# The scans' diagonal and levels 1, 2 and 4 computed between the products of the paired projections

## The chip, the core and the metric

The kernel runs on one core of a Trainium2 chip. A core has five engines that work side by side and wait for each other through semaphores: TensorE (PE in the profile, with its weight loads as PEld), VectorE (DVE), ScalarE (ACT), GpSimd (POOL) and SyncE (SP, which here only issues transfers). TensorE writes into PSUM, eight banks of 128 x 512 floats. Everything else lies in SBUF (128 partitions) or in DRAM. The metric is the time of one execution on the device in microseconds.

## The reference: what is computed

One inference step of a backbone with one layer, over 128 context tokens and 1024 latent tokens (1152 in all), with a model width of 1024. After a normalisation and one input projection there are two branches: a gated linear recurrence in both directions over 8 heads (key and value width 128), and a Fourier mixing of 4 channel groups. Both are gated, projected, merged and projected once more. The part that matters here is the recurrence and what feeds it:

```python
q, ff, fb, vi, zA, u, zB, gA, gB = jnp.split(proj, SPLITS, axis=-1)
qh = jax.nn.silu(heads(q))
logf_f, k_f = forget_gate(heads(ff), lb_f)      # f = lb + (1 - lb) * sigmoid(x), k = 1 - f
logf_b, k_b = forget_gate(heads(fb), lb_b)
o_f, S_f = hgrn2_chunk_scan(qh, logf_f, k_f, vh, s0_f)
o_b_rev, S_b = hgrn2_chunk_scan(qh[:, ::-1], logf_b[:, ::-1], k_b[:, ::-1], vh[:, ::-1], s0_b)
...
S_t = diag(f_t) S_{t-1} + k_t v_t^T,   o_t = S_t^T q_t
```

## The kernel before

**Stages.** Up to about 165 us the input is normalised and split into a high and a low part (three products with reduced operands stand for one product in full precision). Then come, with the v projection ahead, the paired projections: `pair(n, ...)` computes two blocks of 128 output channels for all tokens at once, in Strassen's scheme, with 7 products for 8. After these come the scans, one head after another, mixed with the gated projections of the two branches; then the rest of those and the output projection.

**A pair.** `pair` loads the weights of two blocks (`raw`, 1 MB in two transfers), builds seven operands from them (a11, s1, s2, s3, a12, a22, s4), each split by a cast on ScalarE (L525) and a subtraction on GpSimd (L526); three sums between them run on VectorE (L538 to L546). For each half `j` of the tokens TensorE runs the seven products of 12 matmuls each, 168 in a pair, into banks handed out in turn from six ("doo"), and VectorE adds the products together into `u1`, `u2`, `u3` and the results `ca`, `cb` (L551). What is done with a result depends on the block: `silu` (sigmoid on ScalarE, product on GpSimd), `forget` (sigmoid on ScalarE, L592, then a scale and an offset on GpSimd, L593), `silu_gain` (its product is on VectorE, L588). A transfer of SP takes each result to DRAM: `q_dr`, `f_dr` (both directions of the gate), `gz_dr`, `g_dr` and others. The pairs come in the order u (2 pairs), the heads (16 pairs: q with the forward gate, then the backward gate with zA), zB (2 pairs), gA with gB (7 pairs).

**The Fourier branch between the pairs.** `fourier()` is a generator of 20 steps, each a few small matmuls into the two banks of tag "s" with their copies. `pair` calls one step after each half from the third pair on (L573), so it runs in pairs 3 to 12. The program is written in this order with priorities, and a scheduler places the instructions of each engine; each engine then runs its own list in order.

**The scans.** For each head `load_head` brings the gates `ff` (128 x 2 x 1152) and `q`. `scan_blocks` makes kk = 1 - f and qq = q f, and then the part of the attention inside blocks of 32 tokens, in six steps: the diagonal (m = 0) and the levels m = 1, 2, 4, 8, 16. In a level the halves of kk and qq that belong together are copied side by side by ScalarE into `km` and `qm` (L686, L688); TensorE multiplies them in 36 blocks of 32 x 32 tokens (L695); VectorE merges the result into `a32` under a mask (L700; L698 for the diagonal); and `grow` (L660) multiplies kk and qq by the gates of the neighbouring blocks and joins these gates two by two, in place, in three instructions on VectorE (two of L665, one of L667). `scan_rest` goes on from there with levels 32 and 64, the states `S` from chunk to chunk (L767), the read-out and its norm. `PATTERN` gives the order of steps for each head by letters: E a step of `scan_blocks`, L and Y steps of `scan_rest` of the head before and the one before that, V half a chunk of the late v products, F half a block of the branch projections `dense`. In this stage `matmul` also ties TensorE's list to the order of the program.

Of the kernel before, what the change touches and what calls it, by code (L numbers as in the profile page):

```python
# [11 lines left out]
F32 = mybir.dt.float32  # L12
# [36 lines left out]
PATTERN = ['VVVVEEVVVEVVVEVVEVVEVV', 'LEVLEVLLEVVLLEFEFLLLEF', 'LFEFYYYFLEFLLEFLLEFEFLLLEFF', 'LEYYYFLEFLLEFLLEFEFLLLEFF', 'LEFYYYFLFELLEFLLEFEFLLLEFF', 'LEFYYYFLEFLLEFLLEFEFLLLEFF', 'LEFYYYFLFELLEFLLEFEFLLLEFF', 'ELFYYYFLEFLLEFLLEFEFLLELFF', 'LYYFYFLFLLFLLFLLLFFF', 'YFYYFFF']  # L49
HW = T // 2  # L50
SW = HW // 2
# [9 lines left out]
def diffusion_step(ctx: ExitStack, tc: tile.TileContext, xT, x_tok, w_pr, w_v, w_ada, w_ada_gt,  # L61
# [22 lines left out]
    q_dr = dram.tile([NH, P, T], F32, name="q_dr")  # L84
    f_dr = dram.tile([NH, P, 2, T], F32, name="f_dr")
# [349 lines left out]
    def load_head(p, hd):  # L435
        ff = p.tile([P, 2, T], F32, name="ff")
        nc.sync.dma_start(ff, f_dr[hd])
        q = p.tile([P, T], F32, name="q")
        nc.sync.dma_start(q, q_dr[hd])
        return ff, q  # L440


    def fourier():
        ct = lp.tile([P, T], F32, tag="vt", name="ct")
# [73 lines left out]
    four = fourier()  # L518

    with pool("se", 1) as se, pool("sl", 1) as sl_, pool("sp", 1) as sp:  # L520
# [8 lines left out]
        def pair(n, evacs):  # L529
# [6 lines left out]
            sb = sp.tile([P, 4, P], F32, name="sb")  # L536
# [5 lines left out]
            nc.vector.tensor_tensor(out=sb, in0=a11, in1=a21, op=ALU.subtract)  # L542
            w[7] = split(sb, "s3")
# [9 lines left out]
            for j in range(2):  # L553
                js = slice(j * SW, (j + 1) * SW)
                m = {}
                for i in (1, 5, 6, 7, 4, 2, 3):
                    m[i] = any_ps()[:, :SW]
                    mm3(m[i], [(w[i][0][:, k, :], w[i][1][:, k, :], mov[i][k][0][:, js], mov[i][k][1][:, js])
                               for k in range(4)])
                m1, u1, u2, u3 = (se.tile([P, SW], F32, name=x) for x in ("m1", "u1", "u2", "u3"))  # L560
# [12 lines left out]
                if n > 2:  # L573
                    next(four, None)
# [15 lines left out]
        def forget(i):  # L590
            def ev(c, j):
                nc.scalar.activation(c, c, AF.Sigmoid)  # L592
                nc.gpsimd.tensor_scalar(out=c, in0=c, scalar1=omlb[:, i:i + 1], scalar2=lb[:, i:i + 1], op0=ALU.mult,  # L593
                                        op1=ALU.add)

            return ev
# [27 lines left out]
        yf01 = lp.tile([P, 2, T], F32, tag="ff", name="yf01")  # L624
# [3 lines left out]
        for j in range(1, KT):  # L628
            pair(n, ((sigmoid, g_dr[0, j]), (sigmoid, g_dr[1, j])))
            n += 1  # L630
        first = load_head(lp, 0)
# [28 lines left out]
    def grow(ff, kk, qq, m):  # L660
        kk2, qq2, ff2 = (x.rearrange("p d t -> p (d t)") for x in (kk, qq, ff))
        dims = [[2 * m, T // (2 * m)], [T + m, 2], [1, m]]
        for x, off, step in ((qq2, T + m, -(T + m)), (kk2, m, T - m)):
            xv = view(x, 0, dims)
            nc.vector.tensor_tensor(out=xv, in0=xv, in1=view(ff2, off, [[2 * m, T // (2 * m)], [step, 2], [0, m]]), op=ALU.mult)  # L665
        fv = [view(ff2, o, [[T, 2], [2 * m, T // (2 * m)]]) for o in (0, m)]
        nc.vector.tensor_tensor(out=fv[0], in0=fv[0], in1=fv[1], op=ALU.mult)  # L667

    def scan_blocks(hd, ff, q):
        kk = s0[hd % 2].tile([P, 2, T], F32, name="kk")  # L670
        k0 = s0[0].tile([P, T], F32, tag="km", name="k0", bufs=2)
        qq = s0[hd % 2].tile([P, 2, T], F32, name="qq")
        a32 = s0[hd % 2].tile([P, NCH, 32], F32, name="a32")


        for d in range(2):
            nc.scalar.activation(kk[:, d, :], ff[:, d, :], AF.Identity, bias=ones[:, 0:1], scale=-1.0)
            nc.vector.tensor_tensor(out=qq[:, 1 - d, :], in0=q, in1=ff[:, d, :], op=ALU.mult)  # L678
        nc.vector.tensor_tensor(out=k0, in0=kk[:, 0, :], in1=kk[:, 1, :], op=ALU.add)
        kk2, qq2 = (x.rearrange("p d t -> p (d t)") for x in (kk, qq))  # L680
        for m in (0,) + LEVELS:
            ps = scan_ps()
            if m:
                dims = [[2 * m, T // (2 * m)], [T + m, 2], [1, m]]
                km = s0[0].tile([P, T], F32, name="km", bufs=2)
                nc.scalar.copy(km.rearrange("p (b i m) -> p b i m", i=2, m=m), view(kk2, 0, dims))  # L686
                qm = s0[0].tile([P, T], F32, name="qm", bufs=1)
                nc.scalar.copy(qm.rearrange("p (b i m) -> p b i m", i=2, m=m), view(qq2, 0, dims))  # L688
                grow(ff, kk, qq, m)
            else:  # L690
                km, qm = k0, q
# [10 lines left out]
            if m == 16:  # L702
                heads[hd] = (ff, kk, qq, a32)
# [400 lines left out]
```

## Time and profile before

| what | us |
|---|---|
| median of the runs (3) | 1366.0 |
| lowest and highest | 1364.75, 1376.12 |
| the profiled execution's own time | 1369.38 |
| its span | 1367.6 |
| PE busy in the span | 1257.8 (92%) |
| DVE busy | 853.0 (62%) |
| ACT busy | 569.4 (42%) |
| POOL busy | 658.7 (48%) |

The profile is of one execution on the chip. Each busy time is an average over stages that have different limits, so it is to be read by stage, as the slices of the page show. A row has 40 slices of 34.2 us, each digit is a busy share in tenths (9 is 90% or more), and PEclk is the clock that TensorE was granted, in tenths of full speed.

```profile
PE   5999899999999999999999996878787787999998
DVE  7737744444344344444443478999999999675554
POOL 4426546555647456558643503321312734464654
PEclk8899999999999999999999998898988898999999
```

The paired projections are the slices 5 to 23 or so, the scans 24 to 34. In a row of a timeline the columns are the start and the duration in us, the engine, the line, the operation with output and inputs, and in brackets how long the engine was idle before and what released it. In a row of a group the columns are the count, the busy time, the mean duration of one in ns and the idle time ahead of it. In a row of a tile the three numbers are the shortest, the median and the longest duration in ns. In a row of waits they are the total, the number of waits and the longest. Matmuls overlap, so a duration of 0.29 us stands for a matmul that starts 0.13 us after the one before it.

### The profile page before, as it was taken

The numbers are of one execution on the slowest core, as the hardware profiler recorded it, in microseconds if no ns is written. First come the engines' busy times: TensorE is split into PE (matmuls) and PEld (weight loads), VectorE is DVE, ScalarE is ACT, GpSimd is POOL, SyncE is SP. The second block draws the span as 40 slices with busy tenths as digits, with TensorE's granted clock in tenths as the row PEclk, the third lists the DMA queues.
The fourth block names the chain that finished last, engine by engine and source line by source line (L and its number), as shares of the span: only waits on it lengthen the run. The fifth ranks groups of instructions, "written<-read, shape, count | busy, mean of one in ns | idle before, by whom it ended". The sixth has DMA issues, their size and how long they took to land. (4 is left out here: it accounts for less than half of the span.)

```text
span 1367.6 us, 31165 instructions
## 1 busy us (share of the span) xinstructions
PE 1257.8 (92%) x12768; PEld 1189.8 (87%) x12768; DVE 853.0 (62%) x1403; ACT 569.4 (42%) x1056; POOL 658.7 (48%) x499
## 2 busy tenths in 40 slices
PE   5999899999999999999999996878787787999998
PEld 2679899999999999999999996877786786999886
DVE  7737744444344344444443478999999999675554
ACT  4542223333333233323332446666666664432332
POOL 4426546555647456558643503321312734464654
PEclk8899999999999999999999998898988898999999
DMA  8542242332443443233423243553445433577332
GB/s 321 195 170 73 69 140 84 119 135 91 130 133 117 154 153 114 84 114 109 157 93 113 85 157 107 179 156 113 138 147 172 119 117 100 153 219 234 119 129 99
DMA packets 102993, 185.04 MB, mean 135 GB/s; under 512 B 9777, under 2 KB 70978, under 8 KB 99650
## 3 DMA queue, kind: packets, MB, share of 16 engines
q1 hardware_dynamic: 102562, 182.00, 40.6%
q8 instruction: 100, 1.64, 0.5%
q10 hardware_dynamic: 288, 1.05, 0.3%
q14 instruction: 43, 0.35, 0.1%
HBM read 132.41 MB, written 50.60 MB: 134 GB/s over the span
## 5 line engine op out<-in xcount | busy, mean ns | idle before, releaser
L174 POOL TENSOR_TENSOR w_lo<-w_raw,w_hi 128x512 fp32r<-128x512 f32 (+1 forms) x36 | 78.7, 2188 | 194.3 <-ACT w_hi L172 164.1
L842 POOL TENSOR_TENSOR merged<-merged,gs 128x288 f32<-128x288 f32 x64 | 72.2, 1138 | 65.6 <-DVE gs L841 65.5
L188 PE MATMUL d_ps<-yh,w_hi 128*128 128x288 f32 x256 | 86.7, 339 | 10.7 <-DVE merged L839 4.9
L665 DVE TENSOR_TENSOR qq<-qq,ff 128x1152 f32<-128x1152 f32 x56 | 91.9, 1653 | 6.9 <-ACT qm L688 6.7
L542 DVE TENSOR_TENSOR sb<-raw 128x512 f32<-128x512 f32 x27 | 21.5, 798 | 112.6 <-DMA raw<-in_w_pr 112.6
L665 DVE TENSOR_TENSOR kk<-kk,ff 128x1152 f32<-128x1152 f32 x56 | 89.9, 1605 | 0.3
L188 PE MATMUL d_ps<-yh,w_lo 128*128 128x288 f32 x256 | 80.6, 315 | 0.5 <-POOL w_lo L174 0.5
L188 PE MATMUL d_ps<-yl,w_hi 128*128 128x288 f32 x256 | 80.5, 314 | 0.0
L593 POOL TENSOR_SCALAR c<-c,omlb,lb 128x576 f32<-128x576 f32 x32 | 28.1, 879 | 107.3 <-ACT c L592 60.5
L526 POOL TENSOR_TENSOR a11l<-raw,a11h 128x512 fp32r<-128x512 f32 x27 | 34.9, 1294 | 74.8 <-ACT a11h L525 74.7
L188 PEld LDWEIGHTS d_ps<-yh,w_hi 128*128 128x128 f32 x256 | 52.9, 207 | 13.5 <-ACT w_hi L172 3.9
L551 DVE TENSOR_TENSOR c<-o_ps,u 128x288 f32<-128x288 f32 x108 | 48.9, 453 | 23.4 <-PE o_ps L199 22.0
L584 ACT ACTIVATE sg<-c 128x576 f32<-128x576 f32 x40 | 27.4, 685 | 84.8 <-DVE c L551 82.4
L551 DVE TENSOR_TENSOR u<-o_ps,m 128x288 f32<-128x288 f32 x36 | 16.3, 454 | 74.3 <-PE o_ps L199 70.3
L686 ACT COPY km<-kk 128x1152 f32<-128x1152 f32 x40 | 51.9, 1297 | 14.3 <-DVE kk L665 7.5
L688 ACT COPY qm<-qq 128x1152 f32<-128x1152 f32 x40 | 52.1, 1302 | 10.1 <-PE s_ps L188 7.1
L188 PE MATMUL o_ps<-S,qq 128*128 128x128 f32 x256 | 44.2, 295 | 12.5 <-DVE S L767 12.5
L188 PEld LDWEIGHTS d_ps<-yh,w_lo 128*128 128x128 f32 x256 | 53.0, 207 | 0.9 <-POOL w_lo L174 0.9
L188 PEld LDWEIGHTS d_ps<-yl,w_hi 128*128 128x128 f32 x256 | 53.4, 209 | 0.0
L526 POOL TENSOR_TENSOR s2l<-sa,s2h 128x512 fp32r<-128x512 f32 x27 | 34.9, 1294 | 32.5 <-ACT s2h L525 32.5
L667 DVE TENSOR_TENSOR ff<-ff 128x1152 f32<-128x1152 f32 (+6 forms) x56 | 50.2, 907 | 0.1
L188 PEld LDWEIGHTS s_ps<-qm,km 128*32 128x32 f32 x2880 | 33.0, 123 | 20.0 <-ACT qm L688 14.0
(405 smaller groups left out, 5044.6 us busy)
## 6 DMA issues: line engine op xcount, KB each, us to landing
raw<-in_w_pr SPq DMA_DIRECT2D x52, 512.0 KB, 4.8
gs<-g_dr SPq DMA_DIRECT2D x96, 144.0 KB, 3.1
w_raw<-in_w_pab SPq DMA_DIRECT2D x44, 256.0 KB, 3.2
f_dr<-c SPq DMA_DIRECT2D x32, 288.0 KB, 2.3
ff<-f_dr SPq DMA_DIRECT2D x8, 1152.0 KB, 6.4
wa<-in_w_ada SPq DMA_DIRECT2D x8, 1024.0 KB
g_dr<-c SPq DMA_DIRECT2D x28, 288.0 KB, 2.9
xs<-in_xT SPq DMA_DIRECT2D x6, 768.0 KB, 9.5
```

The lines of the kernel that those rows point to most:

```text
L174: eng.tensor_tensor(out=lo, in0=raw, in1=hi.bitcast(F32), op=ALU.subtract)
L188: queued(nc.tensor.matmul(*args, **kw))
L526: nc.gpsimd.tensor_tensor(out=lo, in0=src, in1=hi.bitcast(F32), op=ALU.subtract)
L542: nc.vector.tensor_tensor(out=sb, in0=a11, in1=a21, op=ALU.subtract)
L551: nc.vector.tensor_tensor(out=out, in0=m, in1=x, op=ALU.add)
L584: nc.scalar.activation(sg, c, AF.Sigmoid)
L593: nc.gpsimd.tensor_scalar(out=c, in0=c, scalar1=omlb[:, i:i + 1], scalar2=lb[:, i:i + 1], op0=ALU.mult, op1=ALU.add)
L665: nc.vector.tensor_tensor(out=xv, in0=xv, in1=view(ff2, off, [[2 * m, T // (2 * m)], [step, 2], [0, m]]), op=ALU.mult)
L667: nc.vector.tensor_tensor(out=fv[0], in0=fv[0], in1=fv[1], op=ALU.mult)
L686: nc.scalar.copy(km.rearrange("p (b i m) -> p b i m", i=2, m=m), view(kk2, 0, dims))
L688: nc.scalar.copy(qm.rearrange("p (b i m) -> p b i m", i=2, m=m), view(qq2, 0, dims))
L842: nc.gpsimd.tensor_tensor(out=out, in0=out, in1=gs, op=ALU.add)
```

## The change

The first four of the six steps of `scan_blocks` (the diagonal and the levels 1, 2 and 4) leave the scans. A new generator `pieces()` computes them for 16 pieces (each head in 640 and 512 tokens) in two tiles `px` and `pz` of fixed place: it loads the gates and q from `f_dr` and `q_dr`, makes kk and qq, does the four steps with the same helpers on 5 or 4 chunks, and writes kk, qq, the joined gates (one of eight, `fa`) and the merged `a32` to DRAM. `pair` now takes steps of `fourier()` and then of `pieces()` after chosen products: two in each half up to pair 7, three from pair 8 on. In the scans `load_head` brings kk, qq, `fa` and `a32`, and only levels 8 and 16 are left of E. Of the rest: the loads of a head are issued one head earlier, into three sets of buffers in turn; the second step of the forget gate moves from GpSimd to ScalarE; the operand s3 is built in place in `raw`; the gA/gB pairs come ahead of the zB pairs; and `PATTERN` is written anew, with V and F between the steps of a head.

```diff
+EARLY = (1, 2, 4)
+LATE = (8, 16)
+GRAN = 8
+PIECES = ((0, 640), (640, T))
-PATTERN = ['VVVVEEVVVEVVVEVVEVVEVV', 'LEVLEVLLEVVLLEFEFLLLEF', 'LFEFYYYFLEFLLEFLLEFEFLLLEFF', 'LEYYYFLEFLLEFLLEFEFLLLEFF', 'LEFYYYFLFELLEFLLEFEFLLLEFF', 'LEFYYYFLEFLLEFLLEFEFLLLEFF', 'LEFYYYFLFELLEFLLEFEFLLLEFF', 'ELFYYYFLEFLLEFLLEFEFLLELFF', 'LYYFYFLFLLFLLFLLLFFF', 'YFYYFFF']
+PATTERN = ['VVVVVVVVEVVE', 'LVVELVVLEVVLVVLVVLFLFLFLF'] + 6 * ['LFEYLFYLFYELFLFLFLFLFL'] + ['LFYLFYLFYLFLFLFLFLFLF', 'YFYFYFF']
...
+    def pieces():
...
+        load(*todo[0])
+        for i, (hd, t0, t1) in enumerate(todo):
...
+            for d in range(2):
+                ds, es = slice(d * w, (d + 1) * w), slice((1 - d) * w, (2 - d) * w)
+                nc.scalar.activation(kk[:, ds], ff[:, ds], AF.Identity, bias=ones[:, 0:1], scale=-1.0)
+                nc.vector.tensor_tensor(out=qq[:, es], in0=q, in1=ff[:, ds], op=ALU.mult)
+            nc.vector.tensor_tensor(out=k0, in0=kk[:, :w], in1=kk[:, w:], op=ALU.add)
+            yield
+            for m in (0,) + EARLY:
+                if m:
+                    halves(kk, k0, m, w)
+                    halves(qq, q, m, w)
+                    grow(ff, kk, qq, m, w)
+                ps = scan_ps()
+                within(ps, k0, q, n, nc.tensor.matmul)
+                merge(a32, m, ps, n)
+                if m == EARLY[-1]:
+                    nc.scalar.copy(fa, ff.rearrange("p (d t) -> p d t", d=2)[:, :, 0:w:GRAN])
+                    nc.sync.dma_start(kk_dr[hd, :, :, t0:t1], kk.rearrange("p (d t) -> p d t", d=2))
+                    nc.sync.dma_start(qq_dr[hd, :, :, t0:t1], qq.rearrange("p (d t) -> p d t", d=2))
...
+                    if i + 1 < len(todo):
+                        load(*todo[i + 1])
+                yield
+    four = chain(fourier(), pieces())
...
+                    if i in (() if n < 3 else (5, 4) if n < 8 else (5, 7, 2)):
+                        next(four, None)
-                if n > 2:
-                    next(four, None)
...
-                nc.gpsimd.tensor_scalar(out=c, in0=c, scalar1=omlb[:, i:i + 1], scalar2=lb[:, i:i + 1], op0=ALU.mult,
-                                        op1=ALU.add)
+                nc.scalar.activation(c, c, AF.Identity, bias=lb[:, i:i + 1], scale=omlb[:, i:i + 1])
...
+    loaded = [first, load_head(s0[0], 1)]
     for n in range(NH + 2):
-        blocks = scan_blocks(n, *(load_head(s2 if n % 2 else lp, n) if n else first)) if n < NH else iter(())
+        if 0 < n < NH - 1:
+            loaded.append(load_head((lp, *s0)[(n + 1) % 3], n + 1, ("kk", "qq", "fa" if (n + 1) % 3 else "tab")))
+        blocks = scan_blocks(n, *loaded[n]) if n < NH else iter(())
```

Where the instructions stand now is seen in the lists of the engines. First TensorE inside a pair of a head, before: the products of the operands s1 and s2 follow one another (t0, t1 are the sums of the tokens' halves, h and l the high and low parts).

```order
L197 MATMUL o_ps<-t0h_811,s1h 128x288
L198 MATMUL o_ps<-t0l_812,s1h 128x288
L199 MATMUL o_ps<-t0h_811,s1l 128x288
L197 MATMUL o_ps<-t1h_838,s2h 128x288
L198 MATMUL o_ps<-t1l_839,s2h 128x288
```

The same place after, with a level of a piece in it (`pz` holds k0 and q side by side, 20 blocks are five chunks).

```order
L206 MATMUL o_ps<-t0h_812,s1h 128x288
L481 MATMUL s_ps<-pz 32x32 x20
L207 MATMUL o_ps<-t0l_813,s1h 128x288
L208 MATMUL o_ps<-t0h_812,s1l 128x288
L206 MATMUL o_ps<-t0h_814,s1h 128x288
```

The blocks of a level now stand in the middle of a product. There are 64 such groups, mostly 29 to 36 product matmuls apart within a piece and 69 to 92 from one piece to the next.

Then VectorE in a pair of a head that makes the backward gate and zA, before.

```order
L588 SCALAR_TENSOR_TENSOR c<-c,small,sg 128x576
L551 TENSOR_TENSOR c<-d_ps,u_6066 128x288
L551 TENSOR_TENSOR u_6176<-d_ps,m_6175 128x288
L540 TENSOR_TENSOR sa<-sa,raw 128x512
L551 TENSOR_TENSOR u_6177<-o_ps,u_6176 128x288
L551 TENSOR_TENSOR c<-o_ps,u_6177 128x288
L551 TENSOR_TENSOR u_6178<-o_ps,u_6176 128x288
```

And after, in such a pair (`px` holds the gates and qq, `ps` the merged result).

```order
L461 TENSOR_TENSOR pz<-pz,px 128x160x2x2
L461 TENSOR_TENSOR px<-px 128x160x2x2
L633 TENSOR_TENSOR u_5578<-d_ps,m_5577 128x288
L463 TENSOR_TENSOR px<-px 128x320
L620 TENSOR_TENSOR sa<-raw 128x512
L633 TENSOR_TENSOR u_5579<-o_ps,u_5578 128x288
L624 TENSOR_TENSOR raw<-raw 128x4x128
L633 TENSOR_TENSOR c<-o_ps,u_5579 128x288
L633 TENSOR_TENSOR u_5580<-o_ps,u_5578 128x288
L474 COPY_PREDICATED ps<-m_i,s_ps 128x160
L461 TENSOR_TENSOR pz<-pz,px 128x80x2x4
```

The additions of the products now alternate with the multiplications of `grow` (L461, L463), and a merge (L474) waits for TensorE in the same list.

Last the queue of SP around a weight load, before.

```order
L572 DMA gz_dr<-c 256x1x288
L533 DMA raw<-in_w_pr 128x1024
L572 DMA f_dr<-c 128x2x288
L533 DMA raw<-in_w_pr 128x1024
L572 DMA f_dr<-c 128x2x288
L572 DMA q_dr<-c 256x1x288
```

And after, from the stores of one piece to the next weight load.

```order
L593 DMA kk_dr<-pz 256x1x640
L594 DMA qq_dr<-px 256x1x640
L595 DMA fa_dr<-ps 128x2x80
L568 DMA px<-f_dr 128x2x512
L569 DMA pz<-q_dr 128x512
L596 DMA fa_dr<-ps 128x160
L656 DMA gz_dr<-c 256x1x288
L656 DMA f_dr<-c 128x2x288
L616 DMA raw<-in_w_pr 128x1024 x2
```

Four stores and two loads of a piece stand ahead of the stores of results and of the next weights, and each waits in the queue for what it moves.

More of the change, by code (lines that the diff above doesn't have):

```diff
@@ L1 @@
 from contextlib import ExitStack, contextmanager
-from itertools import cycle
+from itertools import chain, cycle
 import numpy as np
@@ L516, in fourier, with load @@
                 yield
-    four = fourier()
+    def pieces():
+        x = lp.tile([P, 2, W0], F32, tag="qq", name="px")
+        z = lp.tile([P, 2, W0], F32, tag="kk", name="pz")
+        sm_ = lp.tile([P, 2, 257], F32, tag="tab", name="ps").rearrange("p a b -> p (a b)")
+        todo = [(hd, t0, t1) for hd in range(NH) for t0, t1 in PIECES]
+        def load(hd, t0, t1):
+            w = t1 - t0
+            nc.sync.dma_start(x[:, 0, :2 * w].rearrange("p (d t) -> p d t", d=2), f_dr[hd, :, :, t0:t1])
+            nc.sync.dma_start(z[:, 1, :w], q_dr[hd, :, t0:t1])
+        load(*todo[0])
+        for i, (hd, t0, t1) in enumerate(todo):
+            w, n = t1 - t0, (t1 - t0) // P
+            ff, qq, kk, q, k0 = x[:, 0, :2 * w], x[:, 1, :2 * w], z[:, 0, :2 * w], z[:, 1, :w], z[:, 1, w:2 * w]
+            a32 = sm_[:, :n * 32].rearrange("p (c t) -> p c t", t=32)
+            fa = sm_[:, n * 32:n * 32 + 2 * w // GRAN].rearrange("p (d t) -> p d t", d=2)
+            for d in range(2):
[16 more added lines that the diff above has]
+                    nc.sync.dma_start(qq_dr[hd, :, :, t0:t1], qq.rearrange("p (d t) -> p d t", d=2))
+                    nc.sync.dma_start(fa_dr[hd, :, :FA].rearrange("p (d t) -> p d t", d=2)[:, :, t0 // GRAN:t1 // GRAN], fa)
+                    nc.sync.dma_start(fa_dr[hd, :, FA + t0 // P * 32:FA + t1 // P * 32], sm_[:, :n * 32])
+                    if i + 1 < len(todo):
+                        load(*todo[i + 1])
+                yield
@@ L623, in diffusion_step @@
             n += 2
-        yf01 = lp.tile([P, 2, T], F32, tag="ff", name="yf01")
+        for j in range(1, KT):
+            pair(n, ((sigmoid, g_dr[0, j]), (sigmoid, g_dr[1, j])))
+            n += 1
+        for _ in four:
+            pass
+        yfs = [lp.tile([P, 2, T], F32, tag=t, name="yfs") for t in ("kk", "qq")]
         for g in range(0, NG, 2):
@@ L627, in diffusion_step @@
             n += 1
[L628 to L631, printed above, removed]
+        first = load_head(lp, 0, ("kk", "qq", "tab"))
         tstack.close()
@@ L669, in scan_blocks @@
[L669 to L681, printed above, removed]
-            ps = scan_ps()
[L683 to L691, printed above, removed]
-            for c in range(NCH):
-                for j in range(4):
-                    ts = slice(c * P + 32 * j, c * P + 32 * j + 32)
-                    matmul(ps[32 * j:32 * j + 32, c * 32:c * 32 + 32], lhsT=km[:, ts], rhs=qm[:, ts], start=True, stop=True)
-            pv = ps[:, :NCH * 32].rearrange("p (c t) -> p c t", t=32)
-            if m == 0:
-                nc.vector.tensor_tensor(out=a32, in0=pv, in1=m_d.unsqueeze(1).broadcast_to([P, NCH, 32]), op=ALU.mult)
-            else:
-                nc.vector.copy_predicated(out=a32, mask=m_i[:, LEVELS.index(m), :].unsqueeze(1).broadcast_to([P, NCH, 32]),
-                                          data=pv)
-            if m == 16:
-                heads[hd] = (ff, kk, qq, a32)
@@ new lines, in scan_blocks @@
+    def scan_blocks(hd, kk, qq, fa, a32):
+        kk2, qq2 = flat(kk), flat(qq)
+        for m in LATE:
+            ps = scan_ps()
+            km = s0[0].tile([P, T], F32, name="km", bufs=2)
+            halves(kk2, km, m)
+            qm = s0[0].tile([P, T], F32, name="qm", bufs=1)
+            halves(qq2, qm, m)
+            grow(fa, kk2, qq2, m, g=GRAN)
+            within(ps, km, qm, NCH, matmul)
+            merge(a32, m, ps, NCH)
+            if m == LATE[-1]:
+                heads[hd] = (fa, kk, qq, a32)
@@ L704, in scan_blocks @@
             yield
     def scan_rest(hd):
-        ff, kk, qq, a32 = heads.pop(hd)
-        vt = lp.tile([P, T], F32, tag="vt", name="vt").rearrange("p (c v) -> p c v", v=P)
+        fa, kk, qq, a32 = heads.pop(hd)
+        kk2, qq2 = flat(kk), flat(qq)
+        vt = s1.tile([P, T], F32, name="vt").rearrange("p (c v) -> p c v", v=P)
         nc.sync.dma_start(vt, v_dr[hd])
```

75 lines of the change are left out of this document (46 added, 29 removed).

## The prediction

> **What bounds the kernel now.** I read the busy time of each engine by stage first, because the average over the span mixes stages with different limits. The columns are PE, PEld, DVE, ACT and POOL busy time with instruction counts, then the granted clock, the DMA share and GB/s.
>
> ```profile
> 484.00:806.00 322.00, 321.14 (x2421) 320.68 (x2421) 146.19 (x266) 112.47 (x191) 176.30 (x133) 1.00 0.33 110
> 806.00:1200.00 394.00, 319.95 (x6138) 301.90 (x6137) 359.20 (x519) 237.25 (x449) 135.29 (x79) 0.89 0.46 140
> 1150.00:1200.00 50.00, 42.57 (x486) 41.35 (x487) 33.38 (x70) 23.36 (x71) 28.24 (x21) 0.97 0.44 132
> 1200.00:1250.00 50.00, 48.34 (x350) 47.65 (x349) 33.33 (x56) 15.77 (x27) 30.16 (x31) 0.97 0.81 251
> ```
>
> The paired projections (up to 806 us) are TensorE's: it is busy without a break at full clock, and VectorE has 55% to spare. The scans (806 to 1200 us) are VectorE's: 359 of 394 us, 91%. TensorE stands idle for 74 us there and has a clock of only 0.89, so its work is 319.95 x 0.89 = 285 us at full clock, 72% of the stage. The last two rows show what TensorE reaches when VectorE is filled to two thirds: 42.57 x 0.97 = 41.3 of 50 (83%) with a scan still going on, 48.34 x 0.97 = 46.9 of 50 (94%) with products alone.
>
> Next, the groups of instructions of VectorE in the scans, and one row of the tile kk with its shortest, median and longest duration.
>
> ```profile
> L665 DVE TENSOR_TENSOR qq<-qq,ff 128x1152 f32<-128x1152 f32 x56 | 91.9, 1653 | 6.9 <-ACT qm L688 6.7
> L665 DVE TENSOR_TENSOR kk<-kk,ff 128x1152 f32<-128x1152 f32 x56 | 89.9, 1605 | 0.3
> L700 DVE COPY_PREDICATED a<-m_i,s_ps 128x288 f32<-128x288 int32 x40 | 19.2, 479 | 2.1 <-PE s_ps L188 2.1
> L678 DVE TENSOR_TENSOR qq<-q,ff 128x1152 f32<-128x1152 f32 x14 | 18.8, 1381 | 2.9 <-DMA q<-q_dr 2.9
> L679 DVE TENSOR_TENSOR k<-kk 128x1152 f32<-128x1152 f32 x8 | 14.6, 1820 | 0.0
> L667 DVE TENSOR_TENSOR ff<-ff 128x1152 f32<-128x1152 f32 x8 | 12.8, 1605 | 0.0
> L667 DVE TENSOR_TENSOR ff<-ff 128x576 f32<-128x576 f32 x8 | 11.3, 1408 | 0.0
> L667 DVE TENSOR_TENSOR ff<-ff 128x288 f32<-128x288 f32 x8 | 5.7, 718 | 0.0
> L698 DVE TENSOR_TENSOR a<-s_ps,m_d 128x288 f32<-128x288 f32 x8 | 3.6, 448 | 0.0
> ...
> L665 DVE TENSOR_TENSOR kk<-kk,ff x56: 1328/1353/3007, 810.2 to 1176.7; 128x1152 f32<-128x1152 f32 x56
> ```
>
> Then TensorE's timeline, for what one level costs it and what a wait does to its clock, with the windows over the same stretch.
>
> ```profile
> 960.24 0.83 PE L188 MATMUL s_ps<-qm,km 128*32 128x32 f32 x72
> 961.00 0.40 PE L188 MATMUL d_ps<-yh,w_hi 128*128 128x288 f32 x1
> 961.24 0.29 PE L188 MATMUL d_ps<-yl,w_hi 128*128 128x288 f32 x1
> 961.37 0.30 PE L188 MATMUL d_ps<-yh,w_lo 128*128 128x288 f32 x1
> ...
> 965.38 0.83 PE L188 MATMUL s_ps<-qm,km 128*32 128x32 f32 x72 [2.52 <-ACT qm L688]
> ...
> 967.00 0.44 PE L188 MATMUL d_ps<-yl,w_hi 128*128 128x288 f32 x1
> 967.25 0.44 PE L188 MATMUL d_ps<-yh,w_lo 128*128 128x288 f32 x1
> ...
> 965.00:970.00 5.00, 4.62 (x90) 4.58 (x90) 4.64 (x7) 4.11 (x6) 3.02 (x2) 0.66 0.24 61
> ```
>
> A level of all 1152 tokens takes 960.24 to 961.00, 0.76 us, and the product behind it starts its second matmul after 0.24 instead of 0.13 us, so 0.87 us in all. After a wait of 2.52 us the matmuls follow at 0.24 or 0.25 us instead of 0.13, at a clock of 0.66: here a longer wait of TensorE is paid again behind it.
>
> **The change part by part.**
>
> *A, the scans lose work.* Of the rows above, 24 of 56 in each L665 group (three of seven levels) go, 24 of 40 in L700, and the rest whole: 39.4 + 38.5 + 11.5 + 18.8 + 14.6 + 12.8 + 11.3 + 5.7 + 3.6 = 156 us of VectorE, which leaves 203. TensorE loses 8 heads x 4 steps x 0.87 = 28 us and keeps 257 at full clock. TensorE is late next, and VectorE is no longer the bound. The stage then takes 257 divided by the share that TensorE reaches. The two rows with VectorE at two thirds bound it: 0.83 gives 310 us, 0.94 gives 273. I take 0.87, nearer the first, since the chain of a head stays: 295 us. Gain 99 us (84 to 121).
>
> *B, TensorE's time between the pairs.* The period of a pair without such steps is the distance of the same cast in successive pairs:
>
> ```profile
> 708.05 0.62 ACT L525 CAST a11h<-raw 128x512 fp32r<-128x512 f32 x1 [0.28 <-PE d_ps L198]
> ...
> 774.83 0.62 ACT L525 CAST a11h<-raw 128x512 fp32r<-128x512 f32 x1 [0.29 <-PE d_ps L198]
> ```
>
> These are three pairs, 22.26 us each, of 168 matmuls. A step of 20 or 16 blocks is 0.76 x 20/36 = 0.42 or 0.34 us, 0.38 on the mean, plus 0.11 for the restart: 0.49 us. There are 16 pieces x 4 steps = 64, on an engine with no gap: 31 us, all of it on the path. In the order as built the 64 steps stand between 2654 products, 15.8 pairs, so a pair there takes at least 22.26 + 2 = 24.2 us.
>
> *C, whether VectorE keeps up there.* The windows give 146.19 us over 322/22.26 = 14.5 pairs, 10.1 us a pair. A piece (576 tokens on the mean, half of 1152) adds 9 products of half of 1.353 us (two qq, one k0, six kk and qq), 6.1 us; three ff of 0.68, 0.34 and 0.17; four merges of half of 0.479: 8.3 us clean, so 18.4 of 24.2. Twelve of these instructions read both operands from SBUF. What such an instruction loses next to GpSimd is to be seen in the pairs already:
>
> ```profile
> L546 DVE TENSOR_TENSOR sa<-raw,sa x27: 679/1435/1905, 174.4 to 781.7; 128x512 f32<-128x512 f32 x27
> ...
> 492.06 1.29 POOL L526 TENSOR_TENSOR a22l<-raw,a22h 128x512 fp32r<-128x512 f32 x1
> 492.52 1.38 DVE L546 TENSOR_TENSOR sa<-raw,sa 128x512 f32<-128x512 f32 x1
> ```
>
> The same subtraction takes 0.68 us at its shortest and 1.38 us where it starts inside an instruction of GpSimd. In the scans the mean loss is 1.629 - 1.353 = 0.28 us, at GpSimd's 135/394 = 34%; in the pairs it is 0.75 at the median of L546. With 0.28 the pair needs 18.4 + 3.4 = 21.8 us of VectorE, 90% of 24.2; with 0.75 it needs 27.4, and VectorE would set the pair, 3.2 us more. So the stalls lie between 0 and 15.8 x 3.2 = 51 us. I take 1.6 us a pair, 25 us: VectorE at 91% left TensorE idle for 74 of 394 us (19%) in the scans, and here only 4 steps in 172 instructions wait on that chain, so I take a third of it, 6.5% of 24.2.
>
> The Trainium skill, page "SBUF — State Buffer", section "SBUF: two separate sides", says that VectorE with two SBUF inputs and GpSimd share a port pair as an exclusive lock, and that the loser blocks for the whole instruction. By that rule, were GpSimd found busy each time, a wait is half of a 1.29 us instruction, 0.65 us, the pair needs 26.2 us of VectorE, and C would be 32 us; the trace agrees that it is a wait and not a sharing, 0.68 against 1.38 us. The rule speaks against the change, because it brings the two engines together.
>
> *D, the hand-over.* Head 0's kk and qq take the buffers in which the last pairs multiply by the Fourier result, so they load after that. Ahead of them lie eight half chunks of the late v products, 12 matmuls each.
>
> ```profile
> 806.58 0.27 PE L188 MATMUL d_ps<-vh,h1h 128*128 128x256 f32 x1
> ...
> 808.48 0.28 PE L188 MATMUL d_ps<-vl,h1h 128*128 128x256 f32 x1
> ...
> 955.00:960.00 5.00, 5.00 (x43) 5.00 (x44) 4.98 (x11) 2.31 (x2) 0.00 (x0) 1.00 0.90 284
> ```
>
> Sixteen steps in 1.90 us are 0.119 us a matmul, so the cover is 8 x 12 x 0.119 = 11.4 us. In the queue of SP four other tiles of 1152 KB and a smaller one stand between kk and qq. At 284 GB/s five tiles take 21 us, and with some 4 us for the last evacuation the wait is 14 us; if their buffers are free early it is 0. I take 6, bounded by 0 and 15.
>
> *Edits at nothing.* The forget gate's second step goes from GpSimd to ScalarE:
>
> ```profile
> L593 POOL TENSOR_SCALAR c<-c,omlb,lb 128x576 f32<-128x576 f32 x32 | 28.1, 879 | 107.3 <-ACT c L592 60.5
> L592 ACT ACTIVATE c<-c 128x576 f32<-128x576 f32 x32 | 21.9, 686 | 65.6 <-DVE c L551 51.2 <-issue 14.3
> L686 ACT COPY km<-kk 128x1152 f32<-128x1152 f32 x40 | 51.9, 1297 | 14.3 <-DVE kk L665 7.5
> ...
> raw<-in_w_pr SPq DMA_DIRECT2D x52, 512.0 KB, 4.8
> ...
> 471.40 0.42 SPq L533 DMA_DIRECT2D raw<-in_w_pr  x1
> ...
> 484.06 0.62 ACT L525 CAST a11h<-raw 128x512 fp32r<-128x512 f32 x1 [0.27 <-PE o_ps L198]
> ```
>
> ScalarE is at 112/322 = 35% of the pairs. A piece adds six copies and two activations of half of 1.3 us, 5.2 us, and the gate two of 0.69: it reaches some 60%, and GpSimd is relieved of 28 us. Without that cover the gate would cost 32 x 0.686 = 21.9 us. The DMAs: each head now writes 2.65 MB and reads 1.77 MB more among the pairs, 35 MB over some 400 us, 90 GB/s on top of 110, below the 284 of the row above. The queue of SP holds the weight loads behind the stores of a piece, which wait for VectorE. A weight tile issued at 471.40 lands 4.8 us later and is first cast at 484.06, when TensorE has given the old one free: 7.9 us of slack, which hides a hold-up of that size; beyond it each us of delay costs one. The exchange of the last pairs is hidden under their products.
>
> Sum: -99 + 31 + 25 + 6 = -37 on the profiled execution's 1369.4 us, 1332; it stands 3.4 us above the median of 1366.0, so 1329 for the median.
>
> **The rivals.**
>
> *Full cover.* VectorE fits between the products, C and D are 0: -99 + 31 = -68, 1298 us. For it: 18.4 of 24.2 us clean, and at 484 to 806 us TensorE lost nothing to its neighbours. Against it: the 0.75 of L546.
>
> *VectorE becomes the bound of the pairs (slower).* Place: the twelve two-operand instructions of a piece among seven splits of GpSimd in each pair. It decides from 22.26 + (99 - 6)/15.8 = 28.1 us a pair, that is (28.1 - 18.4)/12 = 0.81 us lost by each; L546 loses 0.75 already, and the evacuations that queue behind it come on top. At 30 us a pair the cost is 15.8 x 7.74 = 122 us: 1366 - 99 + 122 + 6 = 1395. Against it: in the scans they lose 0.28 only, and GpSimd is freed of L593.
>
> *The scans stay bound by the chain of a head.* The cadence of a head is 46.8 us:
>
> ```profile
> 910.30 0.16 DVE L740 COPY tot<-ff 128x18 f32<-128x18 f32 x1
> ...
> 1142.39 0.17 DVE L740 COPY tot<-ff 128x18 f32<-128x18 f32 x1
> PE o_ps L188 <- DVE S L767: 12.5, 6, 5.1
> ...
> 1157.45 0.65 PE L188 MATMUL o_ps<-S,qq 128*128 128x128 f32 x2 [5.08 <-DVE S L767]
> ```
>
> That is 232.1 us for five heads. If waits like those for S (12.5 us in six, the longest 5.1) remain with a free VectorE, the share of TensorE rises only to 0.78: 257/0.78 = 329, gain 65, and 1366 - 65 + 62 = 1363 us, no change. Against it: the stretch from 1150 us holds the longest of these waits, at 1157 us, and still has 0.83.
>
> That the pieces don't run among the products at all is excluded: the last step stands 386 products ahead of the end of the pairs.
>
> **How the numbers follow.** The forecast (gain from A well above B, C and D) has 0.50, full cover 0.18, the chain 0.17, VectorE as the bound 0.15. About 1% (14 us) is what can be told from no change here. Faster by over 1% are the first two, less the edge of the first where A is 84 and C 51: 0.67. Within 1%: the chain and that edge, 0.18. Slower: 0.15. The range reaches down past full cover, to 1290, and up to A 84, C 51 and D 15, 1380; it leaves out most of the slower rival and the corner where A is 121 with no stall at all. The forecast's own range is 1310 to 1352.
>
> **What would show it.** A: the scans from the last pair to the last gz take some 295 us, VectorE near 70%, a clock above 0.93. B and C: pairs of 25.8 us where the steps stand, and little wait of TensorE for k0 or q. C wrong: VectorE above 95% there, products waiting for u and c. D: TensorE's wait ahead of head 0's first level. The forecast is wrong if pairs take 28 us, or a head over 40.

## The result, and the profile after

| | before | after |
|---|---|---|
| median of the runs, us (beside each other) | 1367.95 | 1384.66 (1382.48 to 1387.46) |
| ratio, with 95% interval | | 1.0109 (1.0082 to 1.0136) |
| span of the profiled execution | 1367.6 | 1383.1 |
| pairs end (first late v product) | 806.6 | 904.3 |
| from there to the last gz | 394.6 | 316.6 |
| from there to the end | 166.5 | 162.2 |

The change makes the kernel 1.1% slower, where 1329 us was forecast. The scans win 78.0 us, the paired projections lose 97.7. The windows of the changed kernel (columns as in the prediction), over the sixteen pairs that carry pieces and over the scans in two parts:

```profile
399.82:852.16 452.34, 412.56 (x4983) 397.51 (x4981) 340.43 (x551) 225.55 (x370) 179.16 (x122) 0.97 0.48 156
...
904.31:996.00 91.69, 72.21 (x1068) 68.55 (x1069) 55.95 (x83) 42.96 (x83) 33.54 (x20) 0.89 0.62 211
996.00:1220.91 224.91, 205.60 (x2828) 199.15 (x2818) 148.92 (x319) 116.40 (x306) 80.99 (x69) 0.96 0.61 197
```

Its timeline at the ends of these stretches:

```profile
399.82 0.62 ACT L608 CAST a11h<-raw 128x512 fp32r<-128x512 f32 x1 [0.33 <-PE o_ps L207]
...
852.16 0.61 ACT L608 CAST a11h<-raw 128x512 fp32r<-128x512 f32 x1
...
904.31 0.36 PE L197 MATMUL d_ps<-vh,h1h 128*128 128x256 f32 x1
...
1220.91 0.55 DVE L852 TENSOR_TENSOR gz<-o_ps,gz 128x384 f32<-128x384 f32 x1
```

Sixteen pairs in 452.34 us are 28.3 us each; 25.8 were forecast, and 28 were named as the mark at which the forecast is wrong. Yet VectorE is busy for only 75% there, far from the 95% that I had named for it. The waits of VectorE between 400 and 850 us (total, times, longest, us) show why that mark was no good:

```profile
DVE px L580 <- DMA pz<-q_dr: 29.6, 8, 7.0
DVE pz L461 <- ACT pz L467: 20.1, 17, 2.3
DVE px L580 <- DMA px<-f_dr: 15.0, 3, 6.4
DVE sa L620 <- DMA raw<-in_w_pr: 14.1, 9, 2.2
DVE sa L622 <- POOL s1l L609: 12.9, 9, 2.6
...
DVE u L633 <- PE d_ps L208: 0.2, 1, 0.2
```

All rows of this view add up to 110 us, and with 339 us of work they fill the 450. Under 3 us of the waiting is for TensorE, which is what an engine with time to spare waits for. VectorE's list runs in order, so its waits for transfers and for ScalarE and GpSimd are as full as its work. TensorE's waits over the same stretch:

```profile
PE s_ps L481 <- issue: 18.1, 11, 3.3
PE s_ps L481 <- DVE pz L581: 10.2, 3, 5.3
PE s_ps L481 <- ACT pz L467: 9.0, 11, 2.0
PE d_ps L206 <- DVE u L633: 2.1, 3, 0.9
```

37 of these 39 us stand at the steps of the pieces, 28 of them at the first step of a piece. So the first theory was the hand-over of a piece.

### The profile page after: what moved, and what is told of

The parts are those of the page before. It is cut to its first block, busy times and chain, and to the rows that moved or that the text cites. A ratio compares the mean times of both kernels' runs of the same rounds, so it can differ in the third digit from the quotient of the medians.

```text
span 1383.1 us, 31593 instructions
## 1 busy us (share of the span) xinstructions
PE 1267.5 (92%) x12768; PEld 1191.6 (86%) x12768; DVE 877.9 (63%) x1531; ACT 601.2 (43%) x1168; POOL 611.9 (44%) x467
## 5 line engine op out<-in xcount | busy, mean ns | idle before, releaser
L668 POOL TENSOR_TENSOR c<-c,sg 128x576 f32<-128x576 f32 x24 | 37.2, 1549 | 108.5 <-ACT sg L666 94.4
L481 PEld LDWEIGHTS s_ps<-pz 128*32 128x32 f32 x2304 | 26.3, 113 | 49.7 <-issue 36.5
L481 PE MATMUL s_ps<-pz 128*32 128x32 f32 x2304 | 33.1, 200 | 37.8 <-issue 18.1
L461 DVE TENSOR_TENSOR pz<-pz,px 128x640 f32<-128x640 f32 (+1 forms) x48 | 49.7, 1035 | 21.5 <-ACT pz L467 21.1
L461 DVE TENSOR_TENSOR qq<-qq,fa 128x1152 f32<-128x1152 f32 x32 | 44.8, 1414 | 24.6 <-ACT qm L467 13.3
L580 DVE TENSOR_TENSOR px<-pz,px 128x640 f32<-128x640 f32 (+1 forms) x32 | 27.4, 898 | 48.9 <-DMA pz<-q_dr 29.6
L181 ACT CAST w_hi<-w_raw 128x512 fp32r<-128x512 f32 (+1 forms) x48 | 34.9, 726 | 49.8 <-issue 20.4
L609 POOL TENSOR_TENSOR a12l<-raw,a12h 128x512 fp32r<-128x512 f32 x27 | 41.9, 1553 | 32.0 <-ACT a12h L608 16.8
L461 DVE TENSOR_TENSOR kk<-kk,fa 128x1152 f32<-128x1152 f32 x32 | 52.1, 1644 | 0.7
L674 ACT ACTIVATE c<-c 128x576 f32<-128x576 f32 x32 | 21.9, 686 | 68.3 <-DVE c L633 68.2
```

What stands on the lines that cost most here:

```text
L181: nc.scalar.copy(hi, raw)
L461: nc.vector.tensor_tensor(out=xv, in0=xv, in1=view(ff, off, [[2 * mg, n], [step, 2], [0, m]]), op=ALU.mult)
L481: mm(ps[32 * j:32 * j + 32, c * 32:c * 32 + 32], lhsT=km[:, ts], rhs=qm[:, ts], start=True, stop=True)
L609: nc.gpsimd.tensor_tensor(out=lo, in0=src, in1=hi.bitcast(F32), op=ALU.subtract)
L668: nc.gpsimd.tensor_tensor(out=c, in0=c, in1=sg, op=ALU.mult)
```

## The experiments

The kernel before took 1369.7 to 1375.3 us (medians) beside these runs. Where a run has one time only, I compare the end of the pairs in its trace (806.6 before, 904.3 after).

**First four: the hand-over of a piece.** Theory 1 is the transfer of the next f and q into single buffers; theory 2 is VectorE and GpSimd holding each other up in SBUF; theory 3 is that TensorE's own steps are dearer. e1_no_reload:

```diff
-                    if i + 1 < len(todo):
-                        load(*todo[i + 1])
```

> Every piece after the first works on what lies in the buffers: the transfers of f and q into them are left out, so the output is not the reference's; every instruction of the engines stays. Theory 1 (hand-over of single-buffered pieces: the next f and q are fetched only after the last step of a piece, and TensorE waits for the first level behind it and then runs at a low clock): the pairs with pieces fall from 28.3 to about 25.5 us, 16 x 2.8 = 45 us, about 1338 us. Theory 2 (VectorE and GpSimd hold each other up in SBUF, so that the evacuations and levels come late wherever they stand): pairs stay at 28 us, 1375 to 1385. Theory 3 (TensorE's own steps are simply dearer than the 0.49 us I counted): no change, 1385.

1391.9 us, pairs end at 909.2: no gain at all. Theory 1 falls in this form. Where VectorE no longer waits for transfers it works longer instead; window of that run, and the same window of the changed kernel behind it:

```profile
484.00:806.00 322.00, 286.53 (x3651) 273.36 (x3651) 268.04 (x409) 165.30 (x271) 133.13 (x83) 0.97 0.39 129
```

```profile
484.00:806.00 322.00, 290.31 (x3480) 279.83 (x3479) 237.63 (x392) 160.03 (x265) 124.08 (x86) 0.97 0.49 160
```

268 against 238 us, for 409 and 392 instructions. The pieces are done sooner there (TensorE's last step is at 798 us, not 852), but the 14 pairs that hold them take 29.5 us each. e7_no_blocks:

```diff
-                ps = scan_ps()
-                within(ps, k0, q, n, nc.tensor.matmul)
-                merge(a32, m, ps, n)
+                if m == 0:
+                    nc.vector.memset(a32, 0.0)
```

> The pieces load, prepare, grow and store as before, but their blocks on TensorE and the merges of these are left out (zeros are stored for them), so the output is not the reference's. Theory 1: TensorE has nothing to wait for, neither its 34 us of own steps nor the 40 us of waits at them nor some 30 us of low clock behind: pairs at 22.5 to 23 us, about 1385 - 90 = 1295 us. Theory 2: VectorE still does its nine products a piece beside GpSimd, the evacuations stay late: pairs of 26 to 27 us, 1350 to 1365. Theory 3: only the own steps go, 64 x 0.55 = 35 us: 1350, pairs of 26 us.

1376.6 us, pairs end at 895.3: of 90 us only 9 go, so theories 1 and 3 fall. TensorE now waits for the sums that free its accumulators (waits, 400 to 850 us), and VectorE's products got longer than in the changed kernel (groups of VectorE, first of this run, then of the changed kernel):

```profile
PE o_ps L206 <- DVE u L632: 25.7, 16, 4.6
PE d_ps L206 <- DVE u L632: 21.7, 10, 4.2
```

```profile
L461 DVE TENSOR_TENSOR pz<-pz,px 128x640 f32<-128x640 f32 x24 | 40.2, 1673 | 0.0
```

```profile
L461 DVE TENSOR_TENSOR pz<-pz,px 128x640 f32<-128x640 f32 x24 | 27.5, 1146 | 8.8 <-ACT pz L467 8.5
```

Whichever wait is taken away, the pairs with pieces stay at 27 to 30 us (27.6 here), and VectorE's instructions grow into the room: the 96 products of L461 in the pieces take 96 us in the changed kernel, 109 in e1 and 130 in e7. The other two runs cut the heads into three pieces (`PIECES = tuple((t, t + 384) for t in range(0, T, 384))`), the second with two buffers for f and q and `load(i + 1)` at the start of piece i:

> Three pieces of 384 tokens a head in place of two of 640 and 512, still with one buffer; control for the next run. Theory 1: 24 hand-overs in place of 16, each a little shorter (transfers of 384 and 192 KB): the pairs don't get better, 1380 to 1405 us. Theory 2: the same work of VectorE in smaller instructions: 1385. Theory 3: 96 steps of 12 blocks in place of 64 of 18: a few us more, 1390.

> The same three pieces a head, but f and q have two buffers each, and the next piece's are fetched at the start of a piece. Theory 1: the wait for the transfers goes, as in the run without them: 40 us less than the single-buffered thirds, 1340 to 1355 us. Theory 2 and 3: as the single-buffered thirds, within 10 us.

1488.8 and 1413.5 us. Neither tells anything on the theories: 24 pieces don't find room between the products, and the rest ran bare behind the last pair (in the first, the last pair starts at 878 us and the late v products at 1015).

**Next four: VectorE.** Theory 4 is VectorE's list. Without any pieces (the scans' `kk_dr`, `qq_dr`, `fa_dr` replaced by `f_dr`, `four = fourier()`), and with VectorE's products alone:

> No pieces at all: the diagonal and the levels 1, 2, 4 are computed nowhere, the scans read forget gates in place of the stored tiles (same sizes), so the output is not the reference's. It is the gain of the scans without the price in the pairs. Both theories below: pairs from the tenth on at 22.3 us, the scans as in the changed kernel (317 us), about 1385 - 16 x 5.9 = 1290 us. If the scans' smaller gain hung on the state in which the pairs leave the queues, the scans would be shorter than 317 us here.

> As the run without pieces, but VectorE does its twelve products of each piece at their places, on one piece's buffers: no transfers, no copies of ScalarE, no blocks of TensorE, no merges (output not the reference's). Theory 4 (VectorE's list: its products stand ahead of the sums that free TensorE's accumulators and of the differences that make the next weights): a good part of the price is there with VectorE alone, pairs of 25 to 27 us, 1335 to 1360. Theory 1 in its second form (the chain of a piece over ScalarE, VectorE and TensorE, and TensorE's waits and low clock at its steps): TensorE has nothing to wait for, pairs of 22.5 us, 1290 as without pieces.

1289.3 and 1360.0 us. Without pieces the pairs end at 813.1, 6.5 us later than before (that is the rest of the change in the pairs, the Fourier steps' new places above all as I read it), so the pieces cost 904.3 - 813.1 = 91.2 us. The scans take 312.0 us there, near the 316.6 of the changed kernel, so their length hardly hangs on the pieces. The windows of the run without pieces and of the run with VectorE's products alone:

```profile
400.00:690.00 290.00, 290.00 (x2177) 290.00 (x2176) 125.94 (x243) 112.39 (x188) 136.81 (x101) 1.00 0.32 108
```

```profile
400.00:690.00 290.00, 243.64 (x1654) 236.08 (x1653) 286.68 (x374) 87.38 (x148) 139.13 (x80) 0.94 0.24 79
```

VectorE alone, with no transfer, no copy and no block, moves the end of the pairs to 884.2, 71 us. The pieces stand closer together there than in the changed kernel: from 403 to 691 us, in some ten pairs and not sixteen. TensorE's waits there are those for the sums (400 to 800 us):

```profile
PE o_ps L206 <- DVE u L620: 31.9, 19, 5.1
PE d_ps L206 <- DVE u L620: 14.1, 10, 2.7
```

So VectorE's products alone can make most of such a price, as theory 4 says, and the next question is what makes VectorE's list that long: e8_no_grow leaves out the call of `grow` in the pieces, e9_no_lo has `split` return `hi, hi` from the eighth pair on, without GpSimd's subtraction.

> The pieces as in the changed kernel, but without the nine products by which VectorE grows kk, qq and ff from level to level (the three products at the start of a piece, the merges, ScalarE's copies, the blocks and all transfers stay; output not the reference's). Theory 4: VectorE is relieved of some 9 us a piece, pairs at 24.5 us, 1325 to 1335 us. Theory 1, second form: the transfers, the copies and the waits for them stay, pairs at 26.5 us or more, above 1355.

> From the eighth pair on GpSimd's seven subtractions of a pair that make the low half of a weight are left out, and the high half stands in their place in the same matmuls (output not the reference's). Theory 4 with the shared access to SBUF as its cause: VectorE's products of a piece fall from 0.92 and 1.15 us to some 0.61 and 0.76, pairs at 25 us or less, 1335. Theory 4 by sheer work in the list: VectorE's instructions shrink little, pairs at 27 to 28 us, 1370 to 1385.

1352.8 and 1354.9 us (pairs end at 876.1 and 877.5): each wins about 30 us, between the two answers expected, and 63 and 64 of the 91 us stay. So neither VectorE's products nor GpSimd's halves make the whole price. The second relieves VectorE without taking an instruction from it. Its timeline shows what a product takes alone, and a price that I had wrong:

```profile
408.77 1.42 DVE L461 TENSOR_TENSOR pz<-pz,px 128x640 f32<-128x640 f32 x1
...
413.35 0.82 DVE L461 TENSOR_TENSOR pz<-pz,px 128x640 f32<-128x640 f32 x1
```

The first is the level of 1 token, the second that of 2.

**The two together, and three single parts.** e12 is VectorE's products alone with e9's edit:

> VectorE's products of the pieces alone, as before, and in addition GpSimd's seven low halves of a pair left out from the eighth pair on (the high halves stand in; output not the reference's). If the price of VectorE alone (71 us over the run without pieces) is made by the two engines stretching each other's instructions, it goes nearly away: clean, VectorE needs some 18.5 of 22.3 us, pairs of 22.5 to 23.5 us, 1300 to 1310 us. If it is made by the order of VectorE's list (sums behind products) whatever their length, more than half of it stays: pairs above 24.5 us, 1330 or more.

1301.4 us, pairs end at 823.9: of the 71 us, 11 are left. Its window:

```profile
400.00:600.00 200.00, 192.97 (x1427) 190.33 (x1426) 199.76 (x327) 74.26 (x127) 16.87 (x9) 1.00 0.28 94
```

VectorE is as full as in the run before, 200 of 200 us, and TensorE loses little. So a full list alone isn't the price; the list beside GpSimd is. The 192 products of the pieces take 214 us in e11 and 164 here, and VectorE waits less than 1 us for GpSimd's results in e11, so what GpSimd does there is to make the products long. That the sums come in time behind shorter products is my reading. The Trainium skill, page "SBUF — State Buffer", section "SBUF: two separate sides", has VectorE with two SBUF inputs and GpSimd hold one port pair by turns for whole instructions; by that rule each side loses where the other started first, and the trace agrees: in the run of VectorE alone GpSimd's s1l, 1.36 us in the changed kernel, takes 2.16 us in the mean, all seven halves 1.74 for 1.48.

> The last two pairs don't multiply by the Fourier result (output not the reference's), so that the buffers of the pieces are free two pairs earlier and head 0's kk and qq are fetched before those pairs. If the 19 us that the hand-over costs beyond the steady rate are the wait for head 0's transfers, the stretch from the first late v product to head 0's tot falls from 48 to 35 us or less, about 1370 us. If they are the first head's own chain with no other head beside it, 45 us or more and 1382.

1376.5 us: from the first late v product to head 0's tot 43.1 us, not 35, where the changed kernel has 48.1; to the last gz 308.1 for 316.6. So some 5 of the 19 us of the hand-over are head 0's transfers. The 8.5 us to the last gz tell less: runs that leave this stretch as it is spread from 308.6 (e18) to 317.8 (e1).

> One part of the change undone: the forget gate's second step is GpSimd's again (32 instructions of 0.88 us) and no longer ScalarE's. If VectorE and GpSimd stretch each other, 28 us more of GpSimd beside the pieces make it slower by 5 to 20 us, 1390 to 1405. If ScalarE's copies of the halves are what comes late, it gets faster by some 5 us, 1380.

1382.0 us, no difference that one run can tell. GpSimd's step on the gate, with one tile and two columns as inputs, did no harm to the time that shows; it got longer itself, 1.01 us in the mean for 0.88 in the kernel before. The rule of "28 us more of GpSimd" was too coarse.

> The change for every second head only: pieces for heads 0, 2, 4 and 6, one in two pairs, and heads 1, 3, 5 and 7 computed in the scans from q and f as before (their f and q lie in the buffers that the next early head's kk and qq take); complete computation. If the price comes from VectorE being full, it falls by more than half where VectorE has half of the extra work: 8 pieces at 2.5 us, 20 us, against four heads of the scans at 10 us each, 1340 to 1352 us, faster than both. If the price is the same for each piece (5.7 us), 1366 + 46 - 40 = 1372.

```diff
-        todo = [(hd, t0, t1) for hd in range(NH) for t0, t1 in PIECES]
+        todo = [(hd, t0, t1) for hd in range(0, NH, 2) for t0, t1 in PIECES]
...
+        for m in ((0,) + EARLY if hd % 2 else ()) + LATE:
```

1420.4 us, ratio 1.0371 (1.0341 to 1.0401), slower than both. The pairs end at 864.1, so eight pieces cost 51 us, 6.4 each, as dear as sixteen, 5.7 each (their steps lie between 408 and 713 us, some eleven pairs and not sixteen). And the scans take 393 us, as if no head had been relieved: TensorE waits for the copies of the heads that do all levels there (864 to 1260 us):

```profile
PE s_ps L197 <- ACT km L467: 26.5, 5, 7.9
PE s_ps L197 <- ACT qm L467: 21.5, 10, 4.9
```

**Moving GpSimd's part.** The low halves are made by VectorE instead, from the eighth pair on; first all seven, then three:

```diff
-            nc.gpsimd.tensor_tensor(out=lo, in0=src, in1=hi.bitcast(F32), op=ALU.subtract)
+            eng.tensor_tensor(out=lo, in0=src, in1=hi.bitcast(F32), op=ALU.subtract)
...
+            eng = nc.vector if n >= 8 else nc.gpsimd
```

> From the eighth pair on the seven low halves of a pair are made by VectorE (0.69 us each, 4.8 us a pair more in its list) and no longer by GpSimd (1.29 us or more each); complete computation. If what fills up is the access that the two engines share (GpSimd's 10 us and VectorE's 13 us of a pair one after the other), 4 us of a pair go: pairs of 25 us, 1330 to 1350 us. If it is VectorE's own list, it now holds some 25 us of work a pair: pairs of 28 us or more, 1385 to 1410.

> The same for three of the seven low halves, those of s1, s2 and s4, on which VectorE's next difference waits; complete computation. VectorE has 2.1 us a pair more, the shared access some 2 us less. Shared access as the cause: pairs of 26.5 us, 1350 to 1365. VectorE's own list: pairs of 28.5, 1385 to 1395.

| low halves on VectorE | us | ratio to before | pairs end |
|---|---|---|---|
| 0 (the changed kernel) | 1384.7 | 1.0109 (1.0082 to 1.0136) | 904.3 |
| 3 | 1365.8 | 0.9973 (0.9949 to 0.9996) | 890.3 |
| 7 | 1348.0 | 0.9836 (0.9807 to 0.9865) | 870.1 |

More work in VectorE's list makes the kernel faster, by dose. Window, waits of TensorE (400 to 830 us) and a group of VectorE in the version with seven:

```profile
484.00:806.00 322.00, 311.41 (x3843) 300.18 (x3845) 277.31 (x516) 174.60 (x287) 9.71 (x6) 0.99 0.53 175
```

```profile
PE s_ps L481 <- issue: 7.1, 9, 1.9
PE s_ps L481 <- ACT pz L467: 3.5, 4, 1.1
PE d_ps L206 <- DVE u L634: 2.6, 3, 1.8
```

```profile
L461 DVE TENSOR_TENSOR pz<-pz,px 128x640 f32<-128x640 f32 x24 | 24.7, 1031 | 2.9 <-ACT pz L467 2.8
```

VectorE is at 86% and TensorE's waits fall from 39 to 14 us. Last, the control on the kernel before and three steps on from here: all pairs (`n >= 1`), no reload, and the loads ahead of the stores at the end of a piece.

> Control: the kernel before, with its seven low halves on VectorE from the eighth pair on and nothing else changed; complete computation. Its pairs without Fourier steps are TensorE's at 22.3 us with VectorE at 45%, so the move alone should win little: 1355 to 1368 us. If it wins as much as in the changed kernel (some 36 us), the better version owes nothing to the early levels.

> The changed kernel with the low halves of all pairs on VectorE, those beside the Fourier steps too (GpSimd has these steps' own sums there). If the shared access also makes the Fourier pairs long (24 to 30 us), they fall by 1 to 2 us each over seven pairs: 1335 to 1343 us. If they wait for the Fourier chain, no change from 1348.

> The low halves on VectorE and, as in the first run, no transfers of f and q after the first piece (output not the reference's). With GpSimd out of the way the waits for these transfers (21 us of VectorE over the pairs) should count now: 1325 to 1340 us. If VectorE's list fills the pair by itself (85% busy), 1348 again.

> The low halves on VectorE from the eighth pair on, and at the end of a piece the next piece's f and q are issued ahead of the stores of kk and qq in SP's queue, not behind them; complete computation. If the transfers' wait counts, they land 2 to 3 us sooner for each piece: 1335 to 1345 us. If the stores that now come later hold up the next piece's writes by as much, 1345 to 1352.

The control takes 1369.4 us, ratio 0.9996 (0.9977 to 1.0014): without the early levels the move is worth nothing. Its pairs stay TensorE's; its window, and its first late v product, at 806.58 in the kernel before:

```profile
400.00:600.00 200.00, 200.00 (x1485) 197.59 (x1485) 121.21 (x231) 67.18 (x120) 31.87 (x31) 1.00 0.37 122
```

```profile
805.82 0.28 PE L188 MATMUL d_ps<-vh,h1h 128*128 128x256 f32 x1
```

With all pairs 1344.1 us, ratio 0.9801 (0.9774 to 0.9828); the loads first 1343.8, 0.9809 (0.9770 to 0.9847). Both are about 2% faster than the kernel before; that they beat 1348.0 (1345.12 to 1349.59) isn't certain, and the Fourier pairs stayed at 24 to 28 us. The run without reload takes 1338.9, but its pairs end at 867.9, 2 us earlier: even with GpSimd out of the way the transfers are not the price.

## Why the prediction was wrong, step by step

| term | predicted | measured | from |
|---|---|---|---|
| A, scans | -99 | -96.6 | 298.0 - 394.6 |
| B and C, pieces in the pairs | +56 | +91.2 | 904.3 - 813.1 |
| Fourier steps and the rest of the pairs | 0 | +6.5 | 813.1 - 806.6 |
| D, hand-over | +6 | +18.6 | 316.6 - 298.0 |
| tail | 0 | -4.3 | 162.2 - 166.5 |
| sum, on the profiled spans | -37 | +15.5 | |

*A was right.* TensorE does 72.21 x 0.89 + 205.60 x 0.96 = 262 us of work at full clock in the scans (257 predicted), and in the steady part its share is 205.60 x 0.96 / 224.91 = 0.88 (0.87 predicted): 262/0.88 = 298 us. The scans are no longer VectorE's (149 of 225 us), and after the first a head takes 31 to 38 us. The 316.6 us are split between A and D by this steady share. (In the rival on the chain of a head, 232.1 us for five heads are 46.4 us each, not 46.8; the sum doesn't use it.)

*D was mis-sized:* 18.6 us, above its bound of 15; over the spread of this stretch between runs, 11 to 20. Some 5 us of it are transfers (e6), and most of it is there without any piece (312.0 in e10); that the first head runs with few neighbours is the rest as I read it, and not shown.

*C is where the forecast failed.* The pair takes the time of the rival "VectorE becomes the bound of the pairs", given 0.15: it was to decide from 28.1 us a pair, and the pair takes 28.3. But the price that this rival named, 0.81 us lost by each of a piece's twelve products, is not what happened. The 192 products of the pieces take 184 us in the changed kernel and 156 in e9, without GpSimd's halves, 0.15 us less each. One group of e9, to be set beside the 1146 ns above:

```profile
L461 DVE TENSOR_TENSOR pz<-pz,px 128x640 f32<-128x640 f32 x24 | 24.7, 1028 | 1.5 <-ACT pz L467 0.6
```

VectorE's work came out at 340.43/16 = 21.3 us a pair, near the 21.8 of the prediction's lower case; that is luck, since its clean cost was larger and its loss smaller than put. What that comparison of 21.8 with 24.2 put at nothing is VectorE's own waiting for transfers, ScalarE and GpSimd, 110 us or 6.9 a pair: 21.3 and 6.9 make up the 28.3 of a pair. Two steps behind this failed.

First, "in the scans the mean loss is 0.28": eight of the 56 instructions in that mean are the level of 1 token, which takes 1.7 times as long with no GpSimd near (1.42 against 0.82 us above), so part of that mean was no loss at all. And the three products of the gates were put at 0.68, 0.34 and 0.17 us, where the rows shown (1605, 1408 and 718 ns for a whole head) give half of each, 0.80, 0.70 and 0.36. A piece costs VectorE some 11 us clean, not 8.3.

Second, "only 4 steps in 172 instructions wait on that chain", from which I took a third of what the scans lost. Six of the seven accumulators of half a pair are freed by VectorE's sums, and the next weights hang on its differences, all in one list with the pieces' products and with what these wait for. What holds up a product ahead of a sum holds up TensorE. In the changed kernel this shows at the steps (37 us of waits, and 2 for u), and with no block at all at the sums (47 us of waits for u). Forecasting a share of busy time for VectorE ("above 95%") hid this: at 75% it was full.

GpSimd's halves beside this list are the part of the price that the runs tell apart: 34 us go when VectorE makes them (904.3 - 870.1), 27 when nobody does (e9, where VectorE waits 56 us for q instead). The 57 us that are left are near the 56 forecast for B and C, but 47 of them stand at TensorE's steps, which were put at 31.

*B* can be read where GpSimd is out of the way: TensorE's 64 steps between the products, from the start of the last product ahead to that of the first behind, less 0.13 us, come to 47 us in the version with seven low halves on VectorE and 76 us in the changed kernel; 31 was predicted. The steps themselves were sized well (by the same count those that nothing disturbed took 0.58 and 0.48 us for 20 and 16 blocks, against 0.53 and 0.45), their waits were not.

*The edits at nothing:* the forget gate is one (1382.0 without it). The stores and loads are one too, as far as e1 and e18 tell; the weights' slack was not at stake.

What stays open: how much of e14's gain is the shared access and how much that a low half, made where the next difference is, no longer crosses to another engine; both go with the same edit (the pieces' products fall from 184 to 157 us, and 17.5 us of VectorE's waits for s1l and s2l go). And the 57 us that the pieces still cost in that version (870.1 - 813.1): 47 are at TensorE's steps, and what makes their waits, the rows "issue" above, the profile doesn't say; in e18 TensorE waits there for k0, which VectorE makes at the start of a piece (8.3 us).

## What to carry to other kernels

Work moved "beside" a busy TensorE is free only if the engine that takes it is free in order: ask what each new instruction waits for, what stands behind it in the list, and whether that frees an accumulator. Add up VectorE's work on two SBUF operands and GpSimd's work in a stage: here they took 259 and 178 of the 452 us of the sixteen pairs, and moving GpSimd's share to VectorE won although VectorE is the fuller one (1384.7 to 1348.0 us). The sum alone doesn't decide: in e12 VectorE's two-operand work fills 175 of 200 us by itself, and TensorE loses little. An engine's busy share says little about room: whether it still waits for the engine that should be the bound says it.

## What the runs showed of the hardware

A VectorE product over pairs with runs of one element (the level of 1 token) takes 1.42 us for 640 elements a partition, the same with runs of two or four 0.82. VectorE and GpSimd lengthen each other: the sums that read PSUM kept their 0.45 us in the runs with and without GpSimd's halves, while in the changed kernel single products of two SBUF tiles went from 0.82 or 1.42 up to 2.3 us, and in e11 GpSimd's s1l from 1.3 to 2.2 in the mean. And taking away work elsewhere can lengthen VectorE's instructions: without the blocks a product of the pieces rose from 1.15 to 1.67 us in the mean, with the same seven halves of GpSimd in a pair; why the two met more often is not shown.
